# One written order for TensorE in the scan stage of a two-layer recurrent decoder step

## The chip, the cores and the metric

The kernel runs on one core of a Trainium2 chip. The metric is the device time of one execution in microseconds (us), the median of several runs. Five engines work side by side, each with its own queue of instructions in program order: TensorE (PE, with its weight loads PEld), VectorE (DVE), ScalarE (ACT), GpSimd (POOL) and SyncE (SP, which issues most DMA transfers). An instruction waits in its queue until the semaphores that it needs are set, and whatever stands behind it in that queue waits too.

## The reference

One inference step for 512 prompt tokens and 8 sample sequences of 4 tokens (544 columns) through two layers with model width 1024. Layer 0 runs two mixers on one input projection and joins them in one output projection; layer 1 is an HGRN2 mixer; a gated FFN follows each. The change concerns layer 0's mixers. Mixer A is an RG-LRU: a convolution of width 4, two gates from block-diagonal products, and a linear recurrence, then a product with a gelu:

```
r = sigmoid(einsum(ub, gr_w) + gr_b);  ig = sigmoid(einsum(ub, gi_w) + gi_b)
a = exp(-8 * r * softplus(-lam));      b = sqrt(1 - a*a) * (ig * u)
h_t = a_t * h_{t-1} + b_t;             out_a = gelu(p[..., W_A:P_A]) * h
```

Mixer B is an RWKV-7 with 8 heads of 64: a matrix state per head, whose output goes through a group norm, gets a bonus, and is multiplied by a gate:

```
sk = S kk_t;   S = S * w_t - sk (kk_t a_t)^T + v_t k_t^T;   o_t = S r_t
out_b = (groupnorm(o) * lnx_w + lnx_b + bonus) * (sigmoid(xg) @ g2)
```

The prompt's recurrence begins from zero, the samples' from given states; final states are outputs too.

## The kernel before, in words

A dense product is one TensorE instruction of 128x128 weights on 272 columns; every weight block is split into a high and a low part (`wh`, `wl`; ACT converts `wf` to `wh` at L196, DVE or POOL makes `wl` at L199), so one column of weights takes 8 blocks x 3 products = 24 for each of two halves. SP loads `wf` at L195. All such products are recorded at line 165, the helper `mm`; they are told apart by names: `acc<-xg` for input projections, `acc<-cat` for the output projection.

Mixer 0 first forms its features and scores (not touched). Then comes the scan stage, about 168 to 376 us of the profile. Four kinds of work share it.

The chain: 16 chunks of 32 prompt tokens, one behind the other. A chunk first multiplies the state `Z` by its prepared matrix `wa` (`ch<-Z,wa`), DVE and ACT each copy half of the result back into `Z` (L757, L755), then the products `ch<-Z,TM` make the next state, which DVE adds up (L824) with a decayed copy `sp` that POOL makes (L812); the products `ops` give the outputs. SP loads the chunk's values (L761). The matrices `wa` come from `wyps`, the fold: two chunks in 16 products, copied by DVE or ACT. After each fourth chunk ACT copies the outputs to `o` (L832).

The group norm works on blocks of four chunks: DVE takes sums and a reciprocal root (L848 to L862), ACT a square (L852), POOL scales `o` (L863), TensorE transposes it (`tps`, L868), ACT applies weight and bias (`q<-tps`, L875), DVE adds the bonus, TensorE makes the gate (`gps`), and DVE multiplies.

The samples: `sample()` is a generator. `rpss` products (four pieces of 18 products) read the sample states, `sps` solves, `opss` gives outputs, one small group norm follows, and four `dpss` state products with stores `rS_s` (L954) end it.

The dense filler: four `rglru` tiles, each two columns of weights (96 products), and in the middle four `gate<-uc,gates` products, with ACT's tanh, exp, square and sqrt and DVE's recurrence between (L974 to L1009). ACT's switches of function show as ACT_TABLE_LOAD. `lead(3)` is the first part of the output projection.

The order is written by hand. `PLAN` is a string: `c` steps the scan by one chunk, `s` steps the samples, `g` is the group norm of a block, `f` issues so many filler products, `l` adds the lead, `d` drains the rest. `HOP` gives the filler products in the two halves of each chunk. TensorE's order is held only for products marked `chain=True` (`in_order = "chain"`): chain, folds and dense products; all others (gates, samples, transposes, gate products of the group norm) are placed by the scheduler by priority and by when it thinks their inputs ready. Accumulators in PSUM: three banks `acc`, two for the chain, one for `ops`, two banks `ms_s` for everything else, the folds among them.

Of the kernel before, what the change touches and what calls it, by code (L numbers as in the profile page):

```python
# [15 lines left out]
OP = mybir.AluOpType  # L16
# [38 lines left out]
PLAN = 'c1 f200 s1 c1 c1 s1 c1 c1 s1 c1 s1 c1 g0 c1 s1 c1 s1 c1 c1 s1 c1 g1 s1 c1 c1 l3 c1 c1 c1 g2 c1 c1 f30 c1 d0'  # L55
HOP = (5, 5)
# [66 lines left out]
class Build:  # L123
# [205 lines left out]
    def mixer0(self):  # L329
# [418 lines left out]
        chain = [chp.tile([128, 4, 64], F32, name=f"ch{i}") for i in range(2)]  # L748
        op = self.open("ops0", space=PSUM)
        ms = self.open("ms_s", bufs=2, space=PSUM)  # L750
# [14 lines left out]
        def fold(g, cs):  # L765
            pss = [ms.tile([128, 2, 4, CH], F32, tag="m", name="wyps") for _ in cs]
            for par in range(2):
                for p in range(4):
                    for ps, c in zip(pss, cs):
                        q = quarter(c)  # L770
                        self.mm(ps[:, par, p], AN[q, g, p, 128 * par:128 * par + 128],
                                Yt[q, g, 4 * par + p], chain=True)
            for ps, c in zip(pss, cs):
                wa = z.tile([128, 2, 4, CH], F32, tag="wa", name="wa", bufs=6)
                copy(c % 2, wa, ps)
                folded[4 * g + c] = wa
# [63 lines left out]
        def groupnorm(o, n, blk):  # L840
            assert self.gated
            self.normed.add(blk)
            with tc.high_priority(offset=GN_PRIO):
                normalise(o, n, blk)

        def normalise(o, n, blk):
# [16 lines left out]
            E("g2")(o[:n], o[:n], y[:, :, None].to_broadcast([n, 8, 64]), OP.mult)  # L863
            tps = self.ms.tile([128, 4, 128], F32, tag="m", name="tps")
            cols = slice(128 * blk, 128 * blk + n)
            t = q.rearrange("p a b -> p (a b)").rearrange("p (a b) -> p a b", b=128)
            for p in range(4):
                nc.tensor.transpose(tps[:, p, :n], o[:n, 2 * p:2 * p + 2].rearrange("p a b -> p (a b)"),  # L868
                                    ident[:n, :n])
# [12 lines left out]
        def sample():  # L882
# [25 lines left out]
            def inter(ps, q):  # L908
                for p in range(4):
                    a = diag(p, q)  # L910
                    out = [ps[par][q_rows[par], p] for par in range(2)]
# [9 lines left out]
            rps = [self.ms.tile([64, 4, 64], F32, tag="m", name="rpss") for _ in range(2)]  # L921
            inter(rps, 0)
            for par in range(2):
                r = q_rows[par]
                nc.vector.tensor_copy(rhs[r], rps[par][r])
            yield
            sps = [self.ms.tile([128, 4, 64], F32, tag="m", name="sps") for _ in range(2)]
            for par in range(2):
                for p in range(4):
                    self.mm(sps[par][s_rows[par], p], Yts[q_rows[par], p], rhs[q_rows[par], p])  # L930
                ACT(zc[par][s_rows[par]], sps[par][s_rows[par]], AF.Copy)
            yield
            ops = [self.ms.tile([64, 4, 64], F32, tag="m", name="opss") for _ in range(2)]
            inter(ops, 1)
            o = sm.tile([128, 8, 64], F32, tag="vx", name="o")
            for par in range(2):
                ACT(o[:32, par::2], ops[par][q_rows[par]], AF.Copy)
            yield
            groupnorm(o, 32, 4)
# [17 lines left out]
        def rglru(i):  # L957
# [23 lines left out]
            STT(uc[:, SEQ:].rearrange("p (b s) -> p b s", s=NS), us[:, :, 3:], w, cs, op0=OP.mult, op1=OP.add)  # L981
            tr = rg.tile([128, NT], F32, tag="tr", name="tr")
# [21 lines left out]
            gg = m0.tile([128, SEQ + 7 * NB], F32, tag="d", name="gg", bufs=DB)[:, :NT]  # L1004

            def evg(ps, h, c):
                TT(gg[:, c], ps, rstd()[:, c], OP.mult)
            yield from self.dense_steps([(I["w_in_ab"][4 + i], evg, None)], xg)
# [32 lines left out]
        self.in_order = "chain"  # L1041
        for e in PLAN.split():
# [11 lines left out]
            elif k == "d":  # L1054
                self.drain()
            else:
                groupnorm(obuf[n], 128, n)
# [8 lines left out]
        groupnorm(obuf[3], 128, 3)  # L1066
# [570 lines left out]
```

## Time and profile before

| | before |
|---|---|
| median of 3 runs | 1568.74 us (1566.56 to 1573.54) |
| profiled execution | 1565.48 us |
| its span | 1563.7 us |
| mean granted TensorE clock | 0.97 |
| PE, PEld busy | 1486.7, 1428.4 us (95%, 91%) |
| DVE, ACT, POOL busy | 858.6, 562.7, 417.9 us (55%, 36%, 27%) |
| instructions | 32454 |

Times in the profile count from the start of the span. `x4` is the number of records in a group; one product of 4-byte operands leaves two records. In a row of a timeline the bracket gives the idle time ahead of the group on its engine and what ended it. The granted clock is TensorE's share of its full speed in that stretch.

### The profile page before, as it was taken

Reading aid. Unit: us, or ns where it says so; the run is one execution under the profiler, and the core shown is the slowest. Engines: PE = TensorE matmul, PEld = TensorE weight load, DVE = VectorE, ACT = ScalarE, POOL = GpSimd, SP = SyncE. Lnnn points to the kernel's source line nnn. Section 1 sums busy time; section 2 is a strip of 40 time slices with the busy share of each in tenths; the row PEclk is TensorE's granted clock in tenths of the full one; section 3 lists DMA queues with packets and bytes.
Section 4 is the critical chain, followed back from the end, with each engine's and each line's share of the span. In section 5 each row is a group of like instructions: output and inputs, shape, how many; then the busy total and the mean of one; then the engine's idle time right before and its main releaser. Section 6 shows DMA issues by size and latency. Waiting matters only on the chain.

```text
span 1563.7 us, 32454 instructions
## 1 busy us (share of the span) xinstructions
PE 1486.7 (95%) x13376; PEld 1428.4 (91%) x13376; DVE 858.6 (55%) x1588; ACT 562.7 (36%) x1026; POOL 417.9 (27%) x541
## 2 busy tenths in 40 slices
PE   6998789678999999999999999999999999999998
PEld 6887677568999999999999999999999999999997
DVE  6778735546744344434467667766674443444344
ACT  4644253225533222313353333333453322232234
POOL 4565524441311001101123434434431100110010
PEclk9998879799999999999999999999999999999999
DMA  4221410112222322232242222222332223223221
GB/s 155 68 61 51 139 39 25 37 58 102 74 89 82 95 83 93 84 93 84 86 121 71 84 97 78 84 94 89 113 116 96 88 82 88 98 86 92 85 75 58
DMA packets 87028, 132.68 MB, mean 85 GB/s; under 512 B 24128, under 2 KB 30016, under 8 KB 86752
## 3 DMA queue, kind: packets, MB, share of 16 engines
q1 hardware_dynamic: 86880, 130.60, 26.3%
q8 instruction: 105, 1.72, 0.5%
q14 instruction: 43, 0.35, 0.1%
HBM read 120.07 MB, written 10.50 MB: 83 GB/s over the span
## 4 chain that ended last, share of the span: by engine, by line
PE 84%; DVE 8%; ACT 3%; DMA 2%; issue 1%; POOL 1%; SPq 0%; DVEq 0%; ACTq 0%; POOLq 0%
PE acc L165 73%; PE lv L165 2%; DVE Pd L662 1%; PE ops L165 1%; PE ch L165 1%; PE wyps L165 1%; DVE Y L663 1%; DMA wf<-w_in_ab 1%; DMA wf<-w_out_ab 1%; PE nps L165 1%; PE ds L165 0%; PE rpss L165 0%; PE tr L1452 0%; POOL wl L199 0%; DVE wl L199 0%
## 5 line engine op out<-in xcount | busy, mean ns | idle before, releaser
L165 PE MATMUL acc<-xg,wh 128*128 128x272 f32 x4544 | 886.9, 293 | 15.7 <-ACT xg L256 7.1
L165 PEld LDWEIGHTS acc<-xg,wh 128*128 128x128 f32 x4544 | 722.4, 191 | 27.0 <-ACT xg L256 7.1
L165 PE MATMUL acc<-xg,wl 128*128 128x272 f32 x2272 | 654.2, 294 | 5.2 <-DVE wl L199 2.7
L196 ACT ACTIVATE wh<-wf 128x512 fp32r<-128x512 f32 (+1 forms) x404 | 250.5, 621 | 653.6 <-PE acc L165 520.1
L165 PEld LDWEIGHTS acc<-xg,wl 128*128 128x128 f32 x2272 | 429.7, 191 | 9.3 <-POOL wl L199 3.2
L199 DVE TENSOR_TENSOR wl<-wf,wh 128x512 fp32r<-128x512 f32 (+1 forms) x373 | 268.1, 719 | 188.4 <-ACT wh L196 162.5
L1156 POOL TENSOR_TENSOR S<-S,rstd 128x272 f32<-128x272 f32 x88 | 74.3, 846 | 645.5 <-ACT S L1155 645.4
L165 PE MATMUL acc<-h,wh 128*128 128x272 f32 x1280 | 236.9, 288 | 0.0
L165 PEld LDWEIGHTS acc<-h,wh 128*128 128x128 f32 x1280 | 198.1, 188 | 0.0
L165 PE MATMUL acc<-h,wl 128*128 128x272 f32 x640 | 176.9, 287 | 0.0
L165 PEld LDWEIGHTS acc<-h,wl 128*128 128x128 f32 x640 | 118.3, 189 | 0.0
L1159 DVE TENSOR_TENSOR hh<-acc,S 128x272 f32<-128x272 f32 x88 | 38.8, 441 | 126.5 <-PE acc L165 124.8
L165 PE MATMUL acc<-cat,wh 128*128 128x272 f32 (+2 forms) x512 | 99.9, 295 | 1.9 <-DVE cat L252 1.3
L165 PEld LDWEIGHTS acc<-cat,wh 128*128 128x128 f32 x512 | 82.3, 193 | 3.2 <-DVE cat L252 2.0
L1155 ACT ACTIVATE S<-t 128x272 f32<-128x272 f32 x88 | 37.8, 431 | 124.0 <-DVE t L1154 124.0
L1176 DVE TENSOR_TENSOR x<-acc,x 128x272 f32<-128x272 f32 x80 | 35.0, 439 | 83.2 <-PE acc L165 82.9
L1154 DVE TENSOR_TENSOR t<-acc,rstd 128x272 f32<-128x272 f32 x88 | 38.7, 441 | 71.0 <-PE acc L165 70.9
L165 PE MATMUL acc<-cat,wl 128*128 128x272 f32 (+2 forms) x256 | 73.4, 293 | 0.0
L274 POOL TENSOR_TENSOR ssq<-ssq,sq 128x544 f32<-128x544 f32 x33 | 46.5, 1410 | 87.6 <-ACT sq L273 87.2
L1426 POOL TENSOR_TENSOR K<-K,G 128x256 f32<-128x256 f32 (+1 forms) x48 | 39.5, 823 | 78.2 <-PE lv L165 78.2
L199 POOL TENSOR_TENSOR wl<-wf,wh 128x512 fp32r<-128x512 f32 x31 | 41.9, 1354 | 58.8 <-ACT wh L196 58.0
L165 PEld LDWEIGHTS acc<-cat,wl 128*128 128x128 f32 x256 | 48.9, 193 | 0.0
(346 smaller groups left out, 1556.1 us busy)
## 6 DMA issues: line engine op xcount, KB each, us to landing
wf<-gate SPq DMA_DIRECT2D x88, 256.0 KB, 2.6
wf<-up SPq DMA_DIRECT2D x88, 256.0 KB, 2.9
wf<-down SPq DMA_DIRECT2D x72, 256.0 KB, 2.7
wf<-w_in_c SPq DMA_DIRECT2D x64, 256.0 KB, 2.5
wf<-w_in_ab SPq DMA_DIRECT2D x44, 256.0 KB, 2.8
x<-xT SPq DMA_DIRECT2D x16, 272.0 KB, 5.2
wf<-w_out_ab SPq DMA_DIRECT2D x16, 256.0 KB, 2.5
S<-hS SPq DMA_DIRECT2D x8, 512.0 KB, 6.0
```

The source lines that it names most:

```text
L165: return self.seq(self.nc.tensor.matmul(out, lhsT, rhs, start=start, stop=stop, skip_group_check=True), chain)
L196: nc.scalar.activation(wh[:, :n], wf[:, :n], AF.Copy)
L199: eng.tensor_tensor(wl[:, :n], wf[:, :n], wh[:, :n].bitcast(F32), OP.subtract)
L274: eng.tensor_tensor(self.ssq, self.ssq, t, OP.add)
L662: TT(q, y[:, 0:a, i:i + 1].to_broadcast([P, a, b]), ni.to_broadcast([P, a, b]), OP.mult)
L663: TT(y[:, 0:a, a:], y[:, 0:a, a:], q, OP.add)
L1154: nc.vector.tensor_tensor(t[:, c], ps, rs()[:, c], OP.mult)
L1155: nc.scalar.activation(S[:, c], t[:, c], AF.Silu)
L1156: nc.gpsimd.tensor_tensor(S[:, c], S[:, c], rs()[:, c], OP.mult)
L1159: nc.vector.tensor_tensor(hh[:, c], ps, S[:, c], OP.mult)
L1176: nc.vector.tensor_tensor(x[:, c], ps, x[:, c], OP.add)
L1426: PTT(kv[:, :, 0], kv[:, :, 0], g2[:, :, 1, None].to_broadcast([128, m, b]), OP.mult)
```

## The change

All of it lies in the scan stage.

- `in_order` is "all" instead of "chain": every product of the stage, and now the transposes too, stands on TensorE in the order in which the program issues it.
- `PLAN` and `HOP` are new: 8 filler products in each half chunk instead of 5; before chunk 0 fewer dense products, mixed with single sample pieces; the sample's outputs and state products, one by one, after chunks 2 to 5 and later; output-projection work only behind chunk 15.
- The group norm is split in two at a `yield`: `g` takes statistics and scales, `h` transposes, applies weights and multiplies.
- In an `rglru` tile the second dense column (`gg`) is now issued ahead of the gate products.
- `rpss`, `sps` and `opss` each use one PSUM tile for both halves instead of two, and `inter` yields after each piece.
- The fold's accumulators come from the three `acc` banks; the chain's two banks become one, and `ms_s` has three.

```
-PLAN = 'c1 f200 s1 c1 c1 s1 c1 c1 s1 c1 s1 c1 g0 c1 s1 c1 s1 c1 c1 s1 c1 g1 s1 c1 c1 l3 c1 c1 c1 g2 c1 c1 f30 c1 d0'
-HOP = (5, 5)
+PLAN = 'c1 s1 f80 s1 f30 s1 f30 s1 f25 c1 c1 s1 c1 s1 c1 s1 c1 s1 c1 g0 s1 c1 c1 h0 c1 s1 c1 c1 s1 c1 g1 s1 c1 s1 c1 h1 s1 c1 g2 s1 c1 l3 c1 h2 c1 f20 d0'
+MSB = 3
+HOP = (8, 8)
...
-        chain = [chp.tile([128, 4, 64], F32, name=f"ch{i}") for i in range(2)]
+        both = chp.tile([128, 2, 4, 64], F32, name="ch")
+        chain = [both[:, i] for i in range(2)]
...
-        ms = self.open("ms_s", bufs=2, space=PSUM)
+        ms = self.open("ms_s", bufs=MSB, space=PSUM)
...
-            pss = [ms.tile([128, 2, 4, CH], F32, tag="m", name="wyps") for _ in cs]
+            pss = [self.acc.tile([128, 2, 4, CH], F32, tag="acc", name="wyps", bufs=3) for _ in cs]
...
-                normalise(o, n, blk)
+                yield from normalise(o, n, blk)
...
             E("g2")(o[:n], o[:n], y[:, :, None].to_broadcast([n, 8, 64]), OP.mult)
+            yield
             tps = self.ms.tile([128, 4, 128], F32, tag="m", name="tps")
...
-                nc.tensor.transpose(tps[:, p, :n], o[:n, 2 * p:2 * p + 2].rearrange("p a b -> p (a b)"),
-                                    ident[:n, :n])
+                self.seq(nc.tensor.transpose(tps[:, p, :n], o[:n, 2 * p:2 * p + 2].rearrange("p a b -> p (a b)"),
+                                             ident[:n, :n]))
...
                 for p in range(4):
+                    if p:
+                        yield
                     a = diag(p, q)
-                    out = [ps[par][q_rows[par], p] for par in range(2)]
+                    out = [ps[q_rows[par], p] for par in range(2)]
...
-            rps = [self.ms.tile([64, 4, 64], F32, tag="m", name="rpss") for _ in range(2)]
-            inter(rps, 0)
+            rps = self.ms.tile([64, 4, 64], F32, tag="m", name="rpss")
+            yield from inter(rps, 0)
...
-            sps = [self.ms.tile([128, 4, 64], F32, tag="m", name="sps") for _ in range(2)]
+            sps = self.ms.tile([128, 4, 64], F32, tag="m", name="sps")
...
             STT(uc[:, SEQ:].rearrange("p (b s) -> p b s", s=NS), us[:, :, 3:], w, cs, op0=OP.mult, op1=OP.add)
+            gg = m0.tile([128, SEQ + 7 * NB], F32, tag="d", name="gg", bufs=DB)[:, :NT]
+
+            def evg(ps, h, c):
+                TT(gg[:, c], ps, rstd()[:, c], OP.mult)
+            yield from self.dense_steps([(I["w_in_ab"][4 + i], evg, None)], xg)
...
             nc.gpsimd.tensor_copy(h_sb[:, i], oa[i][:, SEQ - 1::NS])
-            gg = m0.tile([128, SEQ + 7 * NB], F32, tag="d", name="gg", bufs=DB)[:, :NT]
-
-            def evg(ps, h, c):
-                TT(gg[:, c], ps, rstd()[:, c], OP.mult)
-            yield from self.dense_steps([(I["w_in_ab"][4 + i], evg, None)], xg)
             ACT(gg, gg, AF.Gelu_apprx_tanh)
...
-        self.in_order = "chain"
+        self.in_order = "all"
+        halves = {}
...
+            elif k == "g":
+                halves[n] = groupnorm(obuf[n], 128, n)
+                next(halves[n])
             else:
-                groupnorm(obuf[n], 128, n)
+                next(halves[n], None)
```

TensorE's queue where the sample pieces `rpss` of the reading begin, ahead of chunk 0. Before, the second gate set and then all four pieces:

```order
L165 MATMUL acc<-xg,wl 128x272
L165 MATMUL acc<-xg,wh 128x272 x2
L165 MATMUL gate<-uc,gates 128x272 x4
L165 MATMUL rpss<-S_2592,am_2594 32x64 x16
L165 MATMUL rpss<-Zs_2602,Ws_1073 32x64
L165 MATMUL rpss<-Zs_2603,Ws_1074 32x64
L165 MATMUL rpss<-S_2592,am_2596 32x64 x16
```

After, the third of the pieces, with dense products ahead of it and behind it (a product is `L166` now, one line further down):

```order
L166 MATMUL acc<-xg,wl 128x272
L166 MATMUL acc<-xg,wh 128x272 x2
L166 MATMUL rpss<-S_2223,am_2225 32x64 x16
L166 MATMUL rpss<-Zs_2233,Ws_1073 32x64
L166 MATMUL rpss<-Zs_2234,Ws_1074 32x64
L166 MATMUL acc<-xg,wl 128x272
```

The pieces moved apart and forward, in among the dense products; 165 dense products and one gate set stand ahead of chunk 0 instead of 200 and two.

TensorE's queue at the first full group norm (`tps`, `gps`; `ch` is the chain, `wyps` the fold). Before, between the two halves of a chunk:

```order
L165 MATMUL ch_2195<-Z_2178,wa 32x64
L165 MATMUL ch_2195<-Z_2182,wa 32x64
L868 MATMUL tps<-ident,o 128x128 x4
L165 MATMUL gps<-sg,g_237 128x128 x4
L165 MATMUL wyps<-Yt,AN 128x32 x16
L165 MATMUL acc<-xg,wl 128x272
L165 MATMUL acc<-xg,wh 128x272 x2
```

After, behind the second half of chunk 7, and behind a gate set that stands among the fill:

```order
L166 MATMUL ops<-Z_2183,W_1072 32x64 x4
L166 MATMUL acc<-xg,wh 128x272 x2
L166 MATMUL acc<-xg,wl 128x272
L166 MATMUL gate<-uc,gates 128x272 x4
L166 MATMUL acc<-xg,wh 128x272 x2
L166 MATMUL acc<-xg,wl 128x272
L166 MATMUL acc<-xg,wh 128x272 x2
L871 MATMUL tps<-ident,o 128x128 x4
L166 MATMUL gps<-sg,g_237 128x128 x4
L166 MATMUL ch<-Z_2176,wa 32x64
L166 MATMUL ch<-Z_2180,wa 32x64
```

The transposes moved behind more chain work. ACT's queue at that place after (tr and ti are the gates' tanh, a the exp, q the group norm's weighting, `Z_2180` chunk 8's copy):

```order
L1001 ACT_TABLE_LOAD
L1001 ACTIVATE a<-tr,n_182 128x544
L878 ACTIVATE q<-tps,vec 128x128 x4
L1002 ACTIVATE tr<-tr,p_181 128x544
L1004 ACTIVATE uc<-a 128x544
L757 ACTIVATE Z_2180<-ch 32x256
```

The chain's copy stands behind all of these.

TensorE's queue at the end of the scan. Before, behind a late chunk (`tps` and `gps` with cat and xg products between):

```order
L165 MATMUL ops<-Z_2179,W_1071 32x64 x4
L165 MATMUL ops<-Z_2183,W_1072 32x64 x4
L165 MATMUL acc<-xg,wh 128x272
L868 MATMUL tps<-ident,o 128x128 x4
L165 MATMUL acc<-xg,wl 128x272
L165 MATMUL acc<-xg,wh 128x272 x2
```

After, behind chunk 13, where the dense work ends:

```order
L166 MATMUL acc<-xg,wh 128x272 x2
L166 MATMUL acc<-xg,wl 128x272
L166 MATMUL gate<-uc,gates 128x272 x4
L871 MATMUL tps<-ident,o 128x128 x4
L166 MATMUL gps<-sg,g_237 128x128 x4
L166 MATMUL dpss<-vx,TM_1077 64x512 x2
L166 MATMUL ch<-Z_2178,wa 32x64
L166 MATMUL ch<-Z_2182,wa 32x64
```

The last gate set and the second group norm moved behind the dense work, and chunks 14 and 15 follow with nothing between their halves.

More of the change, by code (lines that the diff above doesn't have):

```diff
@@ L920, in inter @@
                                                         zc[par][:, p], start=False, stop=True))
-            rps = [self.ms.tile([64, 4, 64], F32, tag="m", name="rpss") for _ in range(2)]
-            inter(rps, 0)
+            rps = self.ms.tile([64, 4, 64], F32, tag="m", name="rpss")
+            yield from inter(rps, 0)
             for par in range(2):
                 r = q_rows[par]
-                nc.vector.tensor_copy(rhs[r], rps[par][r])
+                nc.vector.tensor_copy(rhs[r], rps[r])
             yield
-            sps = [self.ms.tile([128, 4, 64], F32, tag="m", name="sps") for _ in range(2)]
+            sps = self.ms.tile([128, 4, 64], F32, tag="m", name="sps")
             for par in range(2):
                 for p in range(4):
-                    self.mm(sps[par][s_rows[par], p], Yts[q_rows[par], p], rhs[q_rows[par], p])
-                ACT(zc[par][s_rows[par]], sps[par][s_rows[par]], AF.Copy)
+                    self.mm(sps[s_rows[par], p], Yts[q_rows[par], p], rhs[q_rows[par], p])
+                ACT(zc[par][s_rows[par]], sps[s_rows[par]], AF.Copy)
             yield
-            ops = [self.ms.tile([64, 4, 64], F32, tag="m", name="opss") for _ in range(2)]
-            inter(ops, 1)
+            ops = self.ms.tile([64, 4, 64], F32, tag="m", name="opss")
+            yield from inter(ops, 1)
             o = sm.tile([128, 8, 64], F32, tag="vx", name="o")
             for par in range(2):
-                ACT(o[:32, par::2], ops[par][q_rows[par]], AF.Copy)
+                ACT(o[:32, par::2], ops[q_rows[par]], AF.Copy)
             yield
-            groupnorm(o, 32, 4)
+            yield from groupnorm(o, 32, 4)
             for p in range(4):
@@ L1065, in mixer0 @@
         self.late_pools()
-        groupnorm(obuf[3], 128, 3)
+        for _ in groupnorm(obuf[3], 128, 3):
+            pass
         self.dump("oa0", oa[0], (128, NT))
```

## The prediction

> **What bounds the kernel now.** I read the page's slices first, then the chain that ended last, then a table of windows, the waits in the stretch where the busy share dips, and last the timelines of PE (TensorE) and ACT (ScalarE) there.
>
> ```profile
> PE   6998789678999999999999999999999999999998
> PEclk9998879799999999999999999999999999999999
> ...
> PE acc L165 73%; PE lv L165 2%; DVE Pd L662 1%; PE ops L165 1%; PE ch L165 1%; PE wyps L165 1%; DVE Y L663 1%; DMA wf<-w_in_ab 1%; DMA wf<-w_out_ab 1%; PE nps L165 1%; PE ds L165 0%; PE rpss L165 0%; PE tr L1452 0%; POOL wl L199 0%; DVE wl L199 0%
> ```
>
> One slice is 39 us. From the eleventh slice on TensorE is full: dense products carry 73% of the chain, and no reordering helps there. The dips are slices 1 and 4 to 10; the change touches only the scan, some 190 to 375 us, slices 5 to 10. The windows (length, busy time and count on PE, PEld, DVE, ACT, POOL, granted clock, DMA share, GB/s) say what is to be had:
>
> ```profile
> 190.00:233.00 43.00, 32.89 (x315) 28.14 (x313) 14.47 (x27) 23.87 (x33) 14.02 (x18) 0.77 0.14 48
> 233.00:353.00 120.00, 95.30 (x1347) 76.68 (x1347) 62.46 (x151) 38.06 (x75) 53.45 (x66) 0.87 0.13 39
> 340.00:376.00 36.00, 30.08 (x287) 26.12 (x288) 28.55 (x67) 21.72 (x40) 9.85 (x12) 0.91 0.34 115
> 424.00:820.00 396.00, 396.00 (x3163) 395.92 (x3163) 179.18 (x312) 125.86 (x222) 47.79 (x55) 1.00 0.29 92
> ```
>
> The last row is the price of a dense product when nothing waits: 396/3163 = 0.125 us. In 190 to 353 PE idles 10.1 + 24.7 us, and the granted clock is 0.77 and 0.87. The waits of 182 to 376 (total, times, longest) name the large ones:
>
> ```profile
> ACT Z L755 <- DVE Z L757: 32.1, 14, 5.9
> ...
> PE tps L868 <- POOL o L863: 11.8, 2, 9.6
> ...
> PE ch L165 <- DVE Z L757: 8.2, 3, 7.1
> ```
>
> **The change part by part.** I follow PE in three steps: to the first product of chunk 0, from there to the last evacuation of dense work in the scan, from there to the last group norm's transposes, behind which the order is the old one.
>
> *Step 1, to chunk 0.* PE before (start, length, records, idle ahead and its releaser), then ACT:
>
> ```profile
> 211.10 1.18 PE L165 MATMUL gate<-uc,gates 128*128 128x272 f32 x4 [2.01 <-DVE uc L979]
> ...
> 225.12 1.24 PE L165 MATMUL rpss<-S,am 64*32 64x64 f32 x32
> ...
> 227.09 2.42 PE L165 MATMUL wyps<-Yt,AN 32*128 32x32 f32 x32 [0.50 <-DVE rhss L925]
> ...
> 233.06 1.07 PE L165 MATMUL ch<-Z,wa 128*32 128x64 f32 x16
> ```
>
> ```profile
> 191.96 1.27 ACT L196 ACTIVATE wh<-wf 128x512 fp32r<-128x512 f32 x2 [4.66 <-DMA wf<-w_in_ab]
> 193.24 1.28 ACT L1009 ACT_TABLE_LOAD   x1
> 194.54 0.66 ACT L1009 ACTIVATE gg<-gg 128x544 f32<-128x544 f32 x1
> 195.10 0.47 ACT L989 ACTIVATE tr<-gate,hgr 128x272 f32<-128x272 f32 x1
> ...
> 269.25 0.84 ACT L991 ACTIVATE a<-tr,n 128x544 f32<-128x544 f32 x1
> ...
> 271.91 0.66 ACT L994 ACTIVATE uc<-a 128x544 f32<-128x544 f32 x1
> ...
> 283.36 1.50 ACT L875 ACTIVATE q<-tps,vec 128x128 f32<-128x128 f32 x4 [6.55 <-PE tps L868]
> ```
>
> Before, 200 dense products, two gate sets, four sample pieces and two folds stand ahead of 233.06. After, 165 dense products and one gate set do; 35 and one set go into the scan. Weights landing late hold the start in both orders: ACT ends their conversion at 193.2, and a tanh of 0.47 frees a bank for the fourth gate product at 193.8. Left are 69 products (8.6), two sample pieces (2.5) and switches (0.8): 11.9 us, and 1.5 more at a clock halfway between 0.77 and 1. With folds of 2.42 and of 1.91 (below), chunk 0 starts at 211.5. Between 208 (clock full) and 217 (a gate set still waits 2 us twice) I take that.
>
> *Step 2, the scan.* One chunk with a fold, read as differences of starts:
>
> ```profile
> 243.77 0.64 PE L165 MATMUL ch<-Z,wa 128*32 128x64 f32 x16
> 244.34 1.97 PE L165 MATMUL wyps<-Yt,AN 32*128 32x32 f32 x32
> 246.25 0.39 PE L165 MATMUL acc<-xg,wh 128*128 128x272 f32 x1
> ...
> 247.06 0.68 PE L165 MATMUL ch<-Z,TM 64*64 64x64 f32 x16
> 247.67 0.43 PE L165 MATMUL ops<-Z,W 128*32 128x64 f32 x16
> 248.04 0.52 PE L165 MATMUL acc<-xg,wh 128*128 128x272 f32 x2
> ...
> 248.85 0.64 PE L165 MATMUL ch<-Z,wa 128*32 128x64 f32 x16
> ```
>
> Products with wa 0.57, fold 1.91, five dense 0.81 (so 0.19 for the switch, and eight are 1.19), TM 0.61, outputs 0.37. The other prices, and the large waits:
>
> ```profile
> 282.21 1.11 PE L868 MATMUL tps<-ident,o 128*128 128x128 f32 x4 [9.55 <-POOL o L863]
> ...
> 298.75 1.08 PE L165 MATMUL dpss<-vx,TM 64*64 64x512 f32 x4
> ...
> 302.64 1.07 PE L165 MATMUL dpss<-vx,TM 64*64 64x512 f32 x2 [1.42 <-POOL vx L945]
> ...
> 307.69 0.30 PE L165 MATMUL ch<-Z,wa 128*32 128x64 f32 x2 [1.20 <-DVE Z L824]
> ...
> 317.03 0.66 PE L868 MATMUL tps<-ident,o 128*128 128x128 f32 x4
> ...
> 318.34 0.37 PE L165 MATMUL acc<-xg,wl 128*128 128x272 f32 x1
> ...
> 335.12 1.58 PE L165 MATMUL ch<-Z,TM 64*64 64x64 f32 x16 [7.10 <-DVE Z L757]
> ...
> 350.63 1.08 PE L165 MATMUL gate<-uc,gates 128*128 128x272 f32 x4
> ...
> 374.53 0.65 PE L868 MATMUL tps<-ident,o 128*128 128x128 f32 x4 [2.30 <-POOL o L863]
> ```
>
> After, a chunk costs 0.57 + 1.19 + 0.61 + 0.37 + 1.19 = 3.93. Up to chunk 13, where the dense work runs out, that is 14 chunks less 0.6: 54.4. Beside them 6 folds 11.5, four output pieces of the sample 5.0, two state products 2.2, two gate sets of twice 1.08 4.3, two pairs of tps and gps 2.2 (1.31 at 317.03, less for the short block), sample's sps 0.7, the nearest row being TM's. Sum 80.3.
>
> What goes: 9.55 us, since the statistics of block 0 now run chunks ahead of its transposes; 7.10, a chain copy caught on DVE (VectorE) behind output-projection weights, whose loading moves behind chunk 15; 1.42 and 1.20.
>
> What is new, since nothing may pass a waiting product any more: in the second RG-LRU tile, the fourth gate product finds no bank until table load, gelu and tanh are through (1.28 + 0.66 + 0.47 = 2.4), and sps' second half stands behind table load and exp (1.28 + 0.84, with the handover 2.3): 4.7. In the third, 1.1 for the fourth gate, and chunk 8's copy behind tanh (as exp, 0.84), square (0.66) and four q (1.50), 3.0 less what products cover, 2.4: 3.5. Behind each of them wait chain and dense work alike. Chain copies and additions late on DVE's queue: the wait on DVE's Z was 8.2 in all, 1.1 without the 7.10, and 1.20 stands at 307.69; in the stricter order I take 4, between 0 and 10. Clock: 0.87 before, 1.00 without stalls; 0.93 stretches 80.3 by 6.0. GpSimd (POOL) and SP gain little delay: POOL's sp and am copies move with their chunk, SP's stores of rS_s follow state products that come later. Step 2 is 80.3 + 4.7 + 3.5 + 4 + 6 = 98.5, so it ends at 310.0.
>
> The clock term deserves a look at this row:
>
> ```profile
> 310.00:316.00 6.00, 6.00 (x90) 5.34 (x90) 1.70 (x4) 0.76 (x2) 3.62 (x4) 0.80 0.20 57
> ```
>
> PE is full there, yet granted 0.80 right after idles of only 1.42 and 1.20. So short stalls do cost clock, and I keep the 6.0.
>
> *Step 3, the end.* Chunks 14 and 15 now have no dense work between their halves; what bounds is DVE: group norms 2 and 3, the last RG-LRU tile, cat conversions. Two groups of 340 to 376:
>
> ```profile
> L977 DVE SCALAR_TENSOR_TENSOR cf<-UX,vec,cf 128x568 f32<-128x568 f32 x2 | 2.6, 1324 | 0.2 <-ACT cf L975 0.2
> ...
> L876 DVE TENSOR_TENSOR q<-q,bonus 128x512 f32<-128x512 f32 x1 | 0.7, 691 | 0.1
> ```
>
> From the 28.55 us of that window go the convolution and its evacuations, about 4.2 (2.6 of it L977), which now lie earlier; two sample state additions of that size, 1.4, come in: 25.8. At the window's busy share of 0.79 that is 32.5 us, between 28 (nearly back to back) and 45 (every handover bare, output-projection weights late). PE has two chunks without fill 3.1, a gate set 2.2, two pairs of tps and gps 2.6, a state product 1.1 and 72 cat products 9.0, 18 us of work there, so it waits. The last transposes start at 342.5 instead of 374.53: 32.0 us gained. The profiled execution took 1565.48, 3.3 below the median 1568.74; on the median: 1536.7.
>
> **The rivals.**
> *The clock stays full.* No new stall of step 2 exceeds 2.4 us, against 9.55 and 7.10 before; if only long idles lower the clock, 6.0 goes: 1530.7. For it: the dips of PEclk lie where the long waits are. Against it: the 0.80 above. [...]
>
> *TensorE bound.* Eight products hide every handover: the 12.2 us of stalls and the 6.0 go, and step 3 takes 28: 1536.7 - 12.2 - 6.0 - 4.5 = 1514. For it: at 248.85 the chain went on without a wait behind 0.81 us of dense work. Against it: the two RG-LRU stalls stand in the new order.
>
> *The end eats it.* Step 2's stalls are half as large again (6) and step 3 takes 45: 1555. For it: DVE and ACT have 28.55 + 21.72 us in 36 already. Against it: no fill also means no evacuations.
>
> *Slower.* In a strict order every half chunk waits for its copy or addition with nothing to pass it. If ACT, in its program order of table loads, gates and q, comes later than the eight products cover in each of the 32 halves, each pays. It decides from 32.0/32 = 1.0 us a half; at 1.5, 48 us: 1585. For it: ACT's copy comes only behind DVE's, 14 times and 32.1 us. Against it: of that, PE waited 1.1 us outside the one 7.10.
>
> *The change does nothing:* TensorE's waits are set by the same producers, and the order only renames who waits: 1568.7. Against it: 35 products really move past chunk 0.
>
> **How the numbers follow.** Forecast 0.54 (1525 to 1550 by its own bounds), full clock 0.10, TensorE bound 0.10, the end 0.15, slower 0.07, nothing 0.04. The likeliest gives 1536.7. Left out below 1516 is 0.06, above 1560 some 0.14 (slower, nothing, a bit of the end). A measurement here can tell 0.5%, 7.8 us, from no change: faster 0.54 + 0.10 + 0.10 + 0.12 = 0.86, same 0.04 + 0.03 = 0.07, slower 0.07.
>
> **What would show it.** In the new profile: first ch<-Z,wa near 211.5; tps of block 0 without a wait above 2 us; no ch wait of 7; stalls of 1 to 2.4 us at gate and at sps in the second RG-LRU tile; a clock near 0.93 over the scan; the last tps near 342, with PE waiting on DVE and POOL ahead of it. If that one starts beyond 367, the forecast is wrong, and the waits of ch<-Z on DVE and ACT should say why; if it starts before 325, TensorE was the bound.

## The result, and the profile after

The changed kernel takes 1555.44 us in the median (1553.83 to 1557.07, 4 runs) against 1569.86 for the kernel before on the same chip (1566.56 to 1573.54): a ratio of 0.9908, 95% interval 0.9882 to 0.9933. That is 14.4 us faster, under 1% but clear of the interval. The forecast was 32.0 us faster, 1536.7, with a range of 1516 to 1560: the direction is right, the time lies near the upper end of the range, and the gain is less than half of the one forecast.

The profiled execution took 1554.87 us with a span of 1552.9, 10.8 less than before. The page's slices of the changed kernel, to be laid beside those of before:

```profile
PE   7998788859999999999999999999999999999998
...
PEclk9998988889999999999999999999999999999999
```

TensorE is full from the tenth slice on instead of the eleventh; slices 4 to 9 still have gaps, and the granted clock of slices 6 to 9 is 0.8, where before it swung between 0.7 and 0.9. The three steps of the prediction can be read in PE's timeline (start, length, idle ahead and its releaser):

```profile
211.04 1.07 PE L166 MATMUL ch<-Z,wa 128*32 128x64 f32 x16
...
223.53 0.73 PE L166 MATMUL gate<-uc,gates 128*128 128x272 f32 x2 [1.77 <-ACT tr L999]
...
227.39 1.06 PE L166 MATMUL sps<-rhss,Yts 32*32 32x64 f32 x8 [1.96 <-ACT Zs L936]
...
249.92 1.12 PE L166 MATMUL ch<-Z,TM 64*64 64x64 f32 x16 [2.12 <-ACT Z L757]
...
258.85 0.68 PE L166 MATMUL ch<-Z,TM 64*64 64x64 f32 x16 [2.38 <-ACT Z L757]
...
351.52 1.11 PE L871 MATMUL tps<-ident,o 128*128 128x128 f32 x4 [7.35 <-POOL o L865]
...
363.60 0.66 PE L871 MATMUL tps<-ident,o 128*128 128x128 f32 x4
```

DVE's last evacuation of dense work in the scan, which ends step 2, starts at 326.66:

```profile
326.66 0.44 DVE L990 TENSOR_TENSOR gg<-acc,rstd 128x272 f32<-128x272 f32 x1
```

So chunk 0 starts at 211.04 (forecast 211.5), step 2 ends at 326.66 (310.0), and the last transposes start at 363.60 (342.5; before 374.53). Step 1 came out, step 2 took 115.6 us instead of 98.5, step 3 36.9 instead of 32.5. The windows of these steps (length, busy time and count of PE, PEld, DVE, ACT, POOL, granted clock, DMA share, GB/s):

```profile
211.04:326.66 115.62, 99.11 (x1295) 84.74 (x1294) 63.99 (x143) 42.80 (x78) 48.69 (x61) 0.82 0.11 32
326.66:363.60 36.94, 21.33 (x209) 17.76 (x207) 27.17 (x62) 21.20 (x39) 14.45 (x15) 0.82 0.45 150
```

In step 2 PE is busy for 99.1 us, where the forecast had 80.3 of work at full clock and 6.0 for a lowered one; and it idles 16.5 us, where the forecast had 12.2. The clock is 0.82, not 0.93. Spread evenly over the stretch, the missing 0.18 takes 0.18 x 99.1 = 17.8 us of PE's busy time (an estimate), which fits 99.1 - 80.3 = 18.8. PE's waits in step 2 (total, times, longest):

```profile
PE ch L166 <- ACT Z L757: 10.0, 6, 2.4
PE gate L166 <- ACT tr L999: 3.4, 2, 1.8
PE sps L166 <- ACT Zs L936: 2.0, 1, 2.0
```

The gate and sps waits are those of the forecast, 3.4 + 2.0 = 5.4 us where it had 4.7 and 1.1. The chain's waits for its copies are 10.0 where it had 2.4 and 4. ACT's copy is the last to come, but in most cases ACT is not the late one. Over step 2, ACT's groups show what its copy waits for:

```profile
L757 ACT ACTIVATE Z<-ch 32x256 f32<-32x256 f32 x14 | 5.3, 376 | 29.6 <-DVE Z L759 29.5
```

It waits for DVE's copy at 12 of the 14 chunks, 29.5 us in all, and DVE's timeline ahead of the wait at 249.92 has the group norm's statistics in front:

```profile
246.77 0.69 DVE L855 TENSOR_REDUCE st<-q 128x8 f32<-128x512 f32 x1 [0.70 <-ACT q L854]
...
247.90 0.89 DVE L860 TENSOR_SCALAR st<-st 128x8 int32<-128x8 int32 x1
248.83 0.17 DVE L862 TENSOR_TENSOR st<-st 128x8 f32<-128x8 f32 x1
249.03 0.43 DVE L759 COPY Z<-ch 32x256 f32<-32x256 f32 x1
```

The split of the group norm took the transposes' wait of 9.55 us off TensorE, but its statistics stand on DVE ahead of a copy on which the strict order makes everything wait. At 258.85 the convolution (L982 to L986) stands there instead. Chunk 8 is the exception. Its copy waits in ACT's own queue, as the forecast had it (2.4), behind four q and what follows them there:

```profile
284.42 1.49 ACT L878 ACTIVATE q<-tps,vec 128x128 f32<-128x128 f32 x4
...
287.20 0.38 ACT L757 ACTIVATE Z<-ch 32x256 f32<-32x256 f32 x1
```

```profile
287.63 1.12 PE L166 MATMUL ch<-Z,TM 64*64 64x64 f32 x16 [2.06 <-ACT Z L757]
```

The clock, in windows of 3.4 us, the length of its shortest half-clock stretches (249.8 to 253.2, 260 to 263.4):

```profile
222.50:225.90 3.40, 1.90 (x15) 1.52 (x15) 0.72 (x1) 3.30 (x6) 0.24 (x1) 1.00 0.26 77
225.90:229.30 3.40, 1.91 (x24) 1.65 (x24) 0.17 (x1) 3.17 (x6) 0.00 (x0) 0.51 0.00 0
246.50:249.90 3.40, 1.30 (x11) 1.05 (x8) 2.86 (x9) 0.61 (x2) 2.13 (x4) 0.99 0.30 82
249.90:253.30 3.40, 3.38 (x40) 3.09 (x40) 2.35 (x10) 0.75 (x2) 2.02 (x3) 0.51 0.04 10
253.30:256.70 3.40, 3.18 (x62) 2.63 (x61) 2.55 (x3) 0.74 (x1) 3.32 (x5) 1.00 0.25 67
263.50:266.90 3.40, 3.30 (x59) 2.88 (x55) 2.41 (x6) 1.51 (x4) 1.04 (x1) 1.00 0.00 0
266.90:270.30 3.40, 3.39 (x38) 2.85 (x39) 1.04 (x3) 0.00 (x0) 0.20 (x1) 0.50 0.02 5
```

A window with 1.30 or 1.90 us of work in 3.40 is followed here by one at half clock, and the last pair shows that even a window with 3.30 us of work can precede half clock, one filled mainly with the small products of chain, fold and sample. In the first pair, 1.5 us of idling (3.40 less 1.90) came before 0.51. The reverse does not hold: in step 3, windows with as little work were followed by full clock, and the longest stretch at half clock late in step 2 follows a window that idled 0.6 us:

```profile
300.90:304.30 3.40, 2.79 (x35) 2.47 (x35) 2.55 (x8) 0.99 (x2) 1.48 (x3) 1.00 0.09 19
304.30:314.50 10.20, 9.21 (x82) 8.39 (x80) 9.16 (x23) 3.23 (x9) 5.10 (x6) 0.51 0.12 38
328.35:331.75 3.40, 2.06 (x14) 1.73 (x14) 0.00 (x0) 3.33 (x7) 0.00 (x0) 1.00 0.22 77
331.75:335.15 3.40, 1.65 (x20) 0.70 (x20) 1.84 (x4) 3.40 (x8) 0.94 (x1) 1.00 0.02 5
335.15:338.55 3.40, 2.05 (x36) 1.01 (x36) 3.34 (x6) 2.90 (x5) 1.14 (x2) 1.00 0.21 77
```

So an idle of 1.5 to 2.1 us can bring half clock but need not, and what decides it stays open.

### The profile page after: what moved, and what is told of

It is laid out like the page before. It is cut to its first block, busy times and chain, and to the rows that moved or that the text cites. A ratio compares the mean times of both kernels' runs of the same rounds, so it can differ in the third digit from the quotient of the medians.

```text
span 1552.9 us, 32430 instructions
## 1 busy us (share of the span) xinstructions
PE 1481.4 (95%) x13376; PEld 1427.1 (92%) x13376; DVE 866.5 (56%) x1588; ACT 560.5 (36%) x1024; POOL 419.7 (27%) x541
## 4 chain that ended last, share of the span: by engine, by line
PE 83%; DVE 8%; ACT 4%; DMA 2%; issue 1%; POOL 1%; SPq 0%; DVEq 0%; ACTq 0%; POOLq 0%
PE acc L166 74%; PE lv L166 2%; PE ops L166 1%; DVE Pd L663 1%; PE ch L166 1%; PE wyps L166 1%; DMA wf<-w_in_ab 1%; DVE Y L664 1%; DMA wf<-w_out_ab 1%; PE nps L166 1%; PE ds L166 0%; DVE cf L982 0%; PE tr L1462 0%; ACT wh L197 0%; DVE wl L200 0%
## 5 line engine op out<-in xcount | busy, mean ns | idle before, releaser
L166 PE MATMUL acc<-xg,wh 128*128 128x272 f32 x4544 | 887.7, 293 | 12.0 <-ACT xg L257 6.4
L166 PEld LDWEIGHTS acc<-xg,wh 128*128 128x128 f32 x4544 | 722.5, 191 | 23.3 <-ACT xg L257 7.1
L166 PE MATMUL acc<-xg,wl 128*128 128x272 f32 x2272 | 653.4, 293 | 3.2 <-DVE wl L200 2.7
L166 PEld LDWEIGHTS acc<-xg,wl 128*128 128x128 f32 x2272 | 429.7, 191 | 7.1 <-DVE wl L200 2.9
L166 PE MATMUL acc<-h,wh 128*128 128x272 f32 x1280 | 236.9, 288 | 0.0
L166 PEld LDWEIGHTS acc<-h,wh 128*128 128x128 f32 x1280 | 198.0, 188 | 0.0
L166 PE MATMUL acc<-h,wl 128*128 128x272 f32 x640 | 176.7, 287 | 0.0
L166 PEld LDWEIGHTS acc<-h,wl 128*128 128x128 f32 x640 | 118.1, 188 | 0.0
L166 PE MATMUL acc<-cat,wh 128*128 128x272 f32 (+2 forms) x512 | 97.1, 290 | 0.0
L166 PEld LDWEIGHTS acc<-cat,wh 128*128 128x128 f32 x512 | 80.7, 190 | 0.2
L166 PE MATMUL acc<-cat,wl 128*128 128x272 f32 (+2 forms) x256 | 72.5, 289 | 0.0
L258 DVE SCALAR_TENSOR_TENSOR xg<-x,vec,xg 128x544 fp32r<-128x544 f32 x32 | 38.8, 1213 | 16.8 <-ACT xg L257 16.6
```

Of the source, the lines that this page charges most:

```text
L166: return self.seq(self.nc.tensor.matmul(out, lhsT, rhs, start=start, stop=stop, skip_group_check=True), chain)
L258: nc.vector.scalar_tensor_tensor(act[:, 1], src, g, act[:, 0].bitcast(F32), op0=OP.mult, op1=OP.subtract)
```

## The experiments

Each time is the median of six or more runs; each ratio is to the kernel before, run beside it on the same chip, with its 95% interval. The kernel before took 1565.2 to 1569.9 us on the different chips, so runs of different chips are compared by their ratios. The changed kernel's 0.9908 (0.9882 to 0.9933) is the mark. T is the start of DVE's last evacuation of dense work in the scan.

| run | us | ratio, interval |
|---|---|---|
| e1_pad | 1554.08 | 0.9919 (0.9892 to 0.9945) |
| e2_hop11 | 1553.02 | 0.9903 (0.9873 to 0.9933) |
| e3_gates_first | 1574.95 | 1.0042 (1.0019 to 1.0065) |
| e4_chain | 1544.64 | 0.9855 (0.9826 to 0.9884) |
| e5_gates_later_alone | 1567.13 | 1.0001 (0.9984 to 1.0017) |
| e6_gates_free | 1552.59 | 0.9897 (0.9871 to 0.9924) |
| e8_norm_whole | 1561.46 | 0.9965 (0.9949 to 0.9981) |
| e9_sample_free | 1561.43 | 0.9955 (0.9938 to 0.9973) |
| e10_norm_free | 1557.12 | 0.9919 (0.9890 to 0.9949) |
| e11_copies_act | 1548.97 | 0.9871 (0.9836 to 0.9906) |
| e12_chain_hop7 | 1554.09 | 0.9898 (0.9865 to 0.9930) |
| e13_hop5 | 1552.39 | 0.9893 (0.9859 to 0.9926) |
| e14_act_pad_sps | 1544.65 | 0.9849 (0.9821 to 0.9877) |
| e15_act_sps2 | 1550.07 | 0.9889 (0.9855 to 0.9924) |
| e16_chain_act | 1542.53 | 0.9837 (0.9809 to 0.9866) |
| e17_act_again | 1547.62 | 0.9877 (0.9845 to 0.9908) |

### Is it the clock?

**e1_pad.** Products of real weights with zeros take the place of five idles.

```
+PADS = {4: 17, 5: 19, 8: 16, 11: 8, 12: 14}
...
-                self.fill(HOP[0])
+                self.fill(HOP[0] - 2)
+                self.pads = PADS.get(c, 0)
+                self.fill(2)
...
```

> The changed kernel plus 74 products of real weights with a column of zeros, added into the running dense sum (the result stays the same): 17, 19, 16, 8 and 14 of them ahead of the TM products of chunks 4, 5, 8, 11 and 12, where TensorE idled 2.1, 2.4, 2.1, 1.0 and 1.7 us. They take 74 x 0.125 = 9.3 us, as much as those idles. Theory A (short idles cost clock: after each the granted clock stood at 0.50 for 3.4 us or more): the idles turn into busy time, the half-clock stretches at 250, 260 and 287 to 291 go, each worth 1.7 us, and perhaps the one at 304 to 315: 5 us faster than the changed kernel, about 1550, in spite of 74 more products. Theory B (clock and chain wait are both set by the mix of small products, idles only go with them): the same time or up to 3 us slower, 1555 to 1558, and the half-clock stretches stay.

The stretch from chunk 0 to T, and the windows at 246.5 and 249.9 that the changed kernel had at 0.99 and 0.51:

```profile
246.50:249.90 3.40, 3.40 (x66) 3.07 (x66) 2.58 (x5) 1.71 (x3) 3.06 (x4) 1.00 0.11 24
249.90:253.30 3.40, 3.40 (x53) 3.13 (x51) 3.00 (x13) 0.38 (x1) 1.29 (x3) 1.00 0.25 77
212.95:325.93 112.98, 101.85 (x1369) 88.09 (x1368) 63.79 (x142) 42.57 (x78) 49.50 (x61) 0.88 0.11 32
```

```profile
291.11 0.64 PE L175 MATMUL ch<-Z,wa 128*32 128x64 f32 x16 [1.82 <-DVE Z L845]
294.00 0.68 PE L175 MATMUL ch<-Z,TM 64*64 64x64 f32 x16 [1.06 <-ACT Z L771]
```

Theory A's mechanism holds: with the idle filled, the half clock behind it is gone, and the clock of step 2 rises from 0.82 to 0.88. Its price does not: step 2 is 2.6 us shorter but begins 1.9 later, and the whole is no shorter, the time that theory B had, though B expected the stretches to stay. Where TensorE got faster, it ran into the chain sooner: two waits stand at 291 and 294 that the changed kernel did not have. So in this kernel most of what the better clock gave went into waits for copies and additions that came late anyway.

### Where the copies are late

**e2_hop11** and **e13_hop5** change only the fill of the half chunks.

```
-HOP = (8, 8)
+HOP = (11, 5)      e2_hop11
+HOP = (5, 5)       e13_hop5
```

> The changed kernel with 11 and 5 dense products in the two halves of a chunk instead of 8 and 8. Theory A (the halves with the copies are too short): 3 more products, 0.37 us, off each of the 6 waits for ACT's copy, 2.2 us, and one or two half-clock stretches less: 2 to 5 us faster than the changed kernel, about 1552. Theory C (a copy is late because DVE and ACT work off other things first, by more than the fill can cover, and the second halves then stand bare): 1555 to 1559.

> The changed kernel with 5 dense products in each half chunk, as before the change; 64 or so of them then come behind chunk 15. Theory A (the fill hides the copies): 0.37 us less cover in most of 32 half chunks, up to 12 us more waiting and clock, but chunks 14 and 15 no longer bare (3 to 6 us back), and the last tile's tail stands behind the scan: 5 to 12 us slower than the changed kernel. Rival (the waits come from DVE and ACT queues, whatever the fill): within 3 us of it.

Both are the changed kernel's time within the intervals (0.9903 and 0.9893). e2_hop11 decides between neither of its theories; e13_hop5 lands where its rival expected it. The traces say a little more. PE's waits for ACT's copy in step 2 are 5.8 us in 4 with eleven products, 10.0 in 6 with eight, and 9.7 in 5 with five (in a step 2 that then lasts to chunk 15). Three products more did shorten these waits, but step 3 then took 38.0 us instead of 36.9; three fewer did not lengthen them. How many dense products cover a copy does not decide the time here.

**e11_copies_act.** The copy that DVE made goes to ACT as well.

```
-                        copy(par, zc[par][s_rows[par]], chain[0][s_rows[par]])
+                        copy(1, zc[par][s_rows[par]], chain[0][s_rows[par]])
```

> The changed kernel with both copies of the chain's state products on ACT instead of one on DVE and one on ACT. Theory C (a copy comes late because DVE works off statistics and convolutions first, and ACT's copy only follows DVE's): the eight waits for ACT's copy, 14.0 us, fall to about half: 4 to 8 us faster. Rival (ACT with its table loads and one more copy of 0.38 a chunk is as late): within 3 us of the changed kernel.

PE's waits from chunk 0 to T, and that window:

```profile
PE gate L166 <- ACT tr L999: 3.4, 2, 1.8
PE ch L166 <- ACT Z L757: 2.8, 2, 2.5
PE ch L166 <- DVE Z L826: 2.3, 3, 1.1
PE sps L166 <- ACT Zs L936: 1.9, 1, 1.9
```

```profile
212.47:319.72 107.25, 96.76 (x1295) 83.04 (x1294) 57.00 (x129) 48.17 (x92) 48.34 (x59) 0.83 0.11 32
```

The chain's wait for its copies falls from 10.0 to 2.8 us; its wait for DVE's additions rises from 0.2 to 2.3, so the two together fall from 10.2 to 5.1. Step 2 falls from 115.6 to 107.3, at nearly the same clock. A second run of the same kernel, **e17_act_again**, has 2.8 and 3.7 us of these waits and a step 2 of 109.7. The waits go as theory C expected: most copies were late because of what DVE had in front of them. The totals do not prove its price: the ratios, 0.9871 and 0.9877, lie 5 to 6 us below the changed kernel's, but their intervals overlap with its own.

> The kernel with both copies on ACT once more, beside its variants on the same chip: ratio 0.987 to before again (0.9836 to 0.9906).

### The clock again, where DVE no longer holds the chain

**e14_act_pad_sps** puts 16 products with a column of zeros between the halves of sps, **e15_act_sps2** takes the wait away, both with copies on ACT.

```
                 ACT(zc[par][s_rows[par]], sps[s_rows[par]], AF.Copy)
+                if par == 0:
+                    self.pad(16)                                           e14_act_pad_sps
...
-            sps = self.ms.tile([128, 4, 64], F32, tag="m", name="sps")
+            sps = [self.ms.tile([128, 4, 64], F32, tag="m", name="sps") for _ in range(2)]      e15_act_sps2
...
```

> The kernel with both copies on ACT, plus 16 products with a column of zeros (added into the running dense sum, which they leave as it is) between the two halves of sps, where TensorE idled 1.95 us and the clock then stood at 0.50 from 228 to 239. Theory A (the clock falls by such an idle, and where the chain isn't held up by DVE it costs its whole length): the idle becomes busy time, the half-clock stretch with its 5.1 us goes: from chunk 0 to the last evacuation 102 instead of 107.3 us, 4 to 6 us faster than that kernel. Theory K (half clock in the scan is absorbed by waits that shrink): within 2 us.

> The kernel with both copies on ACT, and sps in two tiles as before the change, so that its second half no longer waits for ACT's copy of the first (1.95 us). Theory A: the wait goes and the half-clock stretch behind it too: 5 to 7 us faster than that kernel. Theory K: 0 to 2 us, the wait moves to the next product.

The 11 us behind sps in e11_copies_act:

```profile
227.80:238.80 11.00, 9.70 (x99) 8.76 (x100) 4.12 (x9) 6.05 (x10) 1.84 (x3) 0.53 0.01 1
```

The same in e14_act_pad_sps, and its step 2:

```profile
231.30:242.30 11.00, 10.94 (x191) 9.78 (x192) 4.17 (x9) 6.62 (x12) 2.79 (x5) 1.00 0.04 9
```

```profile
215.99:318.86 102.87, 93.32 (x1311) 79.68 (x1310) 58.12 (x128) 47.74 (x92) 49.30 (x60) 0.89 0.12 34
```

Step 2 of e15_act_sps2:

```profile
214.78:317.43 102.65, 91.04 (x1295) 77.90 (x1294) 58.13 (x128) 47.71 (x92) 48.09 (x59) 0.89 0.12 33
```

With 16 products more, step 2 is 102.9 us instead of 107.3 (109.7 in e17_act_again), and the 11 us at 0.53 become 11 at full clock: an idle of 1.95 us cost about 0.47 x 11 = 5 us by its clock. In the trace theory A holds in mechanism and price. Of these 4 to 7 us, 3.0 arrive in the total (1544.65 against 1547.62 of e17_act_again on the same chip); that lies between theories A and K, and the intervals overlap. e15's step 2 is as short, yet its total, 1550.07, is 2.5 us longer than that of e17_act_again, outside both theories: step 3 is 39.7 us there, against 35.3 in e11_copies_act, 36.3 in e17_act_again and 35.5 in e14_act_pad_sps. Why the end took back what step 2 gained is not shown. Against the changed kernel, e14's 0.9849 (0.9821 to 0.9877) is 9 us faster with the intervals apart.

### What the parts of the change do

**e3_gates_first** is the changed kernel with the gates ahead of the second dense column again; **e5_gates_later_alone** is the kernel before with nothing changed but that the column comes ahead of the gates. The edit of e3, whose lines go out further up (e5 is the reverse):

```
             nc.gpsimd.tensor_copy(h_sb[:, i], oa[i][:, SEQ - 1::NS])
+            gg = m0.tile([128, SEQ + 7 * NB], F32, tag="d", name="gg", bufs=DB)[:, :NT]
...
+            yield from self.dense_steps([(I["w_in_ab"][4 + i], evg, None)], xg)
             ACT(gg, gg, AF.Gelu_apprx_tanh)
```

> The changed kernel with the gate products ahead of the second dense column again, as before the change. Theory A: the three waits for the fourth gate product (1.8, 1.6, 1.8) and the 2.0 at sps go, but the first gate product now stands behind the convolution (ACT 0.86, DVE 2.2 + 1.4 + 0.2, together 4.8 us) with nothing to pass it, three times some 3 to 4 us: 3 to 8 us slower than the changed kernel, about 1560. Rival: the gelu with its table load ahead of the tanh was the costly part, and with its four waits (7.2 us and two half-clock stretches) gone the time falls to 1546 to 1550.

> The kernel before with one part of the change: the second dense column of an RG-LRU tile ahead of its gate products. Here the scheduler still places the gate products by itself. Theory F (later gate products are a gain by themselves: the convolution's 4.8 us on ACT and DVE lies behind 48 products): the waits for uc (2.0, 1.3) and for banks at 214 to 220 (2.0, 1.1, 1.3) shrink: 4 to 8 us faster than before. Theory G (it is needed only where gates stand in the written order, and is no gain by itself): within 3 us of before, a little slower where the gelu and its table load come ahead of the tanh.

e3: 1.0042, some 21 us slower than the changed kernel and slower than before, with waits of the gates for the convolution:

```profile
189.47 4.03 PE L166 MATMUL gate<-uc,gates 128*128 128x272 f32 x8 [10.50 <-DVE uc L984]
...
214.95 4.00 PE L166 MATMUL gate<-uc,gates 128*128 128x272 f32 x8 [4.23 <-DVE uc L984]
...
230.73 1.07 PE L166 MATMUL ch<-Z,wa 128*32 128x64 f32 x16
```

```profile
321.39 0.82 PE L166 MATMUL gate<-uc,gates 128*128 128x272 f32 x1 [4.31 <-DVE uc L984]
```

Most of the loss stands ahead of the scan: two gate sets now come before chunk 0, and it starts at 230.73 instead of 211.04, 19.7 us later. e5: 1.0001, nothing. Later gates are no gain by themselves; under this plan and one order they are its condition. Theory A of e3 had the sign and under half the size, theory G of e5 holds.

**e8_norm_whole** issues both parts of a group norm at the first one's place.

```
                 next(halves[n])
+                next(halves[n], None)
```

> The changed kernel with both parts of each group norm issued at the first one's place. TensorE's written order then holds chain and dense work behind transposes that wait for about 9 us of statistics (9.55 in the kernel before), at blocks 0, 1 and 2. Theory A (each such wait is paid whole, the split is what makes one order possible): 3 x 7 to 9 us, 20 to 28 us slower than the changed kernel. Rival (the chain has that much slack, DVE and ACT bound it anyway): 5 to 10 us slower.

0.9965: 9 us slower than the changed kernel, the rival's size. But the waits that both theories speak of do not come: in this trace the transposes of blocks 0, 1 and 2 start without an idle in front. For block 0, DVE had ended the statistics at 252, and the transposes start at 261.86. What grows in step 2 is the chain's wait for its copies, 12.9 us instead of 10.0, and a dense product waits 2.6 us for a statistic on DVE. What the split spares at the transposes is therefore not measured by this run.

**e4_chain, e6_gates_free, e9_sample_free, e10_norm_free** take all, or one class, of the newly ordered products out of the written order.

```
-        self.in_order = "all"
+        self.in_order = "chain"        e4_chain
...
-        if self.in_order == "all" or chain and self.in_order == "chain":
+        if not self.free and (self.in_order == "all" or chain and self.in_order == "chain"):
...
+                    self.free = True                    e6_gates_free (around the gate products; e9 around the sample's steps, e10 around tps and gps)
                     self.mm(ps[:, :HF], gate_w[:, q, i], uc[:, c])
+                    self.free = False
```

> The changed kernel with TensorE's order held only for chain, folds and dense products, as before the change. Theory A (the written order of samples, gates and transposes is worth something by itself, the rest comes from the new plan): the scheduler puts gates and transposes back where it thinks them ready, waits of 2 to 7 us come back at a few places: 1558 to 1565. Rival: the plan and the fill do it all and the strict order only adds waits (gate and sps, 7.2 us and their clock): 1545 to 1552.

> The changed kernel with the gate products alone taken out of TensorE's written order and left to the scheduler. Theory D (the 8 us between this order and the one for chain, folds and dense products alone lie at the gates, which stand ahead of chain and dense work while ACT does a table load, a gelu and the tanh): the three waits of 1.6 to 1.8 and part of the clock go: 5 to 8 us faster than the changed kernel. Theory E (they lie at the sample's products, sps and the output pieces, which the plan spreads over the chunks one by one): within 3 us of the changed kernel.

> The changed kernel with the sample's products alone (rpss, sps, opss, dpss and its short group norm) taken out of TensorE's written order. Theory E (the cost of the full order lies at the sample's products): 5 to 8 us faster than the changed kernel, with the wait of 2.0 at sps gone. Theory D (it lies at the gates): 0 to 3 us faster, the sps wait alone.

> The changed kernel with the group norm's transposes and gate products alone taken out of TensorE's written order. Gates free and sample free each left the time of the changed kernel or made it longer, all three free made it 8 us shorter. Theory H (the cost of the full order lies at the group norm, above all at block 2's transposes, 7.35 us): 5 to 8 us faster than the changed kernel. Theory J (no single class carries it; it is the end of the scan, where with all of them free the last tile and block 2 come earlier, 21 us from the last evacuation to the last transposes against 37): within 3 us of the changed kernel.

e4: 0.9855, 8 us faster than the changed kernel. Its steps 2 and 3:

```profile
220.93:333.83 112.90, 100.57 (x1321) 82.10 (x1321) 71.63 (x161) 50.93 (x92) 52.37 (x64) 0.86 0.15 44
333.83:354.84 21.01, 16.05 (x181) 14.89 (x178) 15.14 (x37) 8.73 (x17) 10.65 (x10) 0.72 0.54 177
```

Chunk 0 starts 9.9 us later, step 2 is 2.7 shorter, and step 3 takes 21.0 us instead of 36.9: with samples and group norms ahead, DVE has 15.1 us of work left there, not 27.2. Theory A of e4 falls, and its rival holds in the number: the strict order gives part of the plan's gain back. It does not do so where the rival put it, at the gates and sps, but in step 3. No class by itself does it: gates free 0.9897 and group norm free 0.9919 can't be told from the changed kernel, samples free 0.9955 is 7 us slower. Theories D, E and H fall, J stands as far as it says that no class carries it. Which pair does it, or whether all three are needed, stays open.

**e12_chain_hop7** and **e16_chain_act** build on e4: fill of 7, and both copies on ACT.

```
-        self.in_order = "all"
+        self.in_order = "chain"
...
-HOP = (8, 8)
+HOP = (7, 7)                                                       e12_chain_hop7
...
-                        copy(par, zc[par][s_rows[par]], chain[0][s_rows[par]])
+                        copy(1, zc[par][s_rows[par]], chain[0][s_rows[par]])       e16_chain_act
```

> The changed kernel with the order held for chain, folds and dense products alone, and 7 dense products in each half chunk instead of 8, so that they last to chunk 15. Theory J (the end is where time is to be had): the waits of 3.3, 1.8 and 3.2 us at chunks 14 and 15 go, 3 to 6 us faster than the same order with 8 (ratio 0.9855 to before): 0.982. Rival (the last tile comes two chunks later and DVE's end work moves behind it): 0.986 to 0.990.

> Both copies on ACT together with the order held for chain, folds and dense products alone. Each was faster than the changed kernel by itself, 6 and 8 us. If they act at different places (copies in the scan, free gates and samples at its end): ratio to before about 0.981, 1537. If the second only removes the same waits: 0.985, as the order alone.

e12: 0.9898, its rival's number: T comes at 349.76 instead of e4's 333.83 and the last transposes at 361.55 instead of 354.84. That the last RG-LRU tile does it was argued and not isolated; one wait of the chain for ACT's copy alone takes 9.3 us there. e16: 0.9837, 26 us faster than before and the fastest median of all, nearer to the second number of its expectation than to the first. The intervals of e4 and e16 overlap, so whether copies on ACT add anything to the looser order is not shown.

## Why the prediction was right in sign and wrong in size

*What held.* The gain comes from the scan, and the identical order behind the last transposes carries it to the end: those start 10.9 us earlier, the span is 10.8 shorter. The waits that were to go (9.55, 7.10) went. The waits that were to come at the fourth gate product, at sps and at chunk 8's copy came: 1.77, 1.96 and 2.06 us. Step 3 was mostly DVE's, 27.2 us of work (forecast 25.8) in 36.9 (32.5): from 334.2 to 350.3 it was busy for 15.6 of 16.2 us, and the 7.35 us at block 2's transposes end just behind that. The first 7.5 us of the step, though, were ACT's, which was busy for 7.4 of them with the last tile's gelu, gates, exp and table loads.

*What was luck.* Step 1 came out to half a microsecond, 211.04 for 211.5, by two errors that cancel. The fourth gate product started at 192.83 instead of 193.8 and the folds at 205.03 instead of 207.2, since the clock was full there; the folds then took 6.0 us instead of 4.3, with a wait of 1.13 and half clock.

*What failed: the clock term of step 2.* "0.93 stretches 80.3 by 6.0" took the middle between two clocks, above the 0.87 of before. It was 0.82 (before, from chunk 0 to T, 0.88), and PE was busy 99.1 us, 12.8 more than the forecast's 86.3. The prediction had the row at hand in which short idles came before a low clock, and still let the new stalls leave the clock better. 0.18 x 115.6 / 0.5 makes some 42 us of step 2 at half clock. Half of it goes with the new stalls of 1.7 us and more: 226 to 236.2, 249.8 to 253.2, 260 to 263.4 and 287.3 to 290.7, 20.4 us. The rest (to 215.7, 267 to 273.8 and 304.3 to 314.5) follows windows of 3.4 us in which PE idled only 1.1, 0.1 and 0.6 us, and why the clock fell there stays open. With copies on ACT, e14 shows the price of one such idle: 1.95 us, and about 5 more of clock. The 12.8 us are not what a full clock would have gained in the changed kernel: e1 raised it to 0.88, and its total stayed the same.

*What failed second: the chain's waits.* They were 10.2 us (10.0 for copies, 0.2 for additions), not 4 + 2.4. Chunk 8's 2.06 is the term of 2.4; the 4 became 8.1, since DVE works off statistics and convolutions ahead of a copy. The forecast took this risk from waits in a kernel whose order let other products pass. It also read the 7.10 of before as a copy behind output-projection weights on DVE. The weights were at the root, but on ACT, which waited 4.9, 3.1 and 1.0 us for them. On DVE a statistic stood in front of the copy, and it waited for ACT's copy of the outputs:

```profile
333.92 0.69 DVE L848 TENSOR_REDUCE st<-o 128x8 f32<-128x512 f32 x1 [7.49 <-ACT o L832]
334.64 0.43 DVE L757 COPY Z<-ch 32x256 f32<-32x256 f32 x1
```

So the mechanism that then cost the new order time, a copy behind statistics in DVE's queue, was there to be read. e11, which takes the copies off DVE, halves the 10.2 us. Step 3's 4.4 us are the last part; 12.8 + 4.3 + 4.4, less 0.5 of step 1, is the 21 us between 342.5 and 363.6.

In the total, e14 shows that late DVE copies, the idle at sps and the clock behind it are together worth 9 us of the 17.6 that were missing. The rest is read from the trace and not shown by a run.

*The rivals.* "The end eats it" gave 1555, the time that came, but by luck: its clock was still 0.93, and its end took 45 us where 36.9 were measured; its longer stalls in step 2 were nearly right (some 18 us, 16.5 measured). "The clock stays full" fell with the clock at 0.82. "TensorE bound" fell with PE idle for 16.5 us in step 2 and 15.6 in step 3. "The change does nothing" fell with the interval of the ratio. "Slower" did not come: late copies are its mechanism, at six halves in step 2 and not at 32.

## What to carry to other kernels

Price a stall on TensorE with the clock that it may cost, not by its own length alone (e14 filled an idle of 1.95 us, worth an estimated 5 us more by its clock): look at the granted clock in windows of a few microseconds around each idle. One written order moves the risk to the engines that feed it (here 10.0 us of waits for copies in step 2); before fixing it, look for what stands ahead of each copy in the other queues. When several parts are changed together, try the order and the parts apart: here a looser order with the same plan was faster, and a part without worth by itself (gates later) was what the strict order needed. Where two waits feed each other, as a low clock and late copies do here, removing one alone may give nothing (e1: the clock of step 2 at 0.88 instead of 0.82, new waits of 1.82 and 1.06 us, a ratio of 0.9919 against 0.9908).

## What the runs showed of the hardware

From 190 to 376 us of the changed kernel, TensorE's granted clock stood at 0.50 in eight stretches: 209 to 215.7, 226 to 236.2, 249.8 to 253.2, 260 to 263.4, 267 to 273.8, 287.3 to 290.7, 304.3 to 314.5 and 342 to 355.6. They lasted 6.7, 10.2, 3.4, 3.4, 6.8, 3.4, 10.2 and 13.6 us. 16 products put into one idle of 1.95 us turned 0.53 (e11) into 1.00 (e14) over the 11 us behind it. Idles of this length do not always bring half clock: the windows from 328.35 and 331.75, with 2.06 and 1.65 us of work in 3.40, were followed by full clock (1.00). A window full of small products can also precede half clock (263.5 to 266.9, with 3.30 us of work in 59 records, then 0.50); which property of them counts was not tried.
